# Expert activations of 48 tokens from gathered rows of u, those of 208 from dense products

## The chip, the cores and the metric

One core of one Trainium2 chip. The metric is the device time of one execution in microseconds (us), as a median of several runs. A profiled execution on the same core gives the trace.

## The reference

Two transformer blocks on 256 tokens of width 2048 (`D`), all in fp32. The change concerns the last part, the expert layer of the second block. For each token and each of 8 heads it picks 16 of 16384 experts (128 in all), and an expert is a row of `u_table` and a row of `v_table`, each of 2048 numbers:

```python
q = jnp.dot(h, w_pq)                      # per head two halves, scored against 128 keys each
v1, i1 = lax.top_k(s1, 16); v2, i2 = lax.top_k(s2, 16)
vals, ci = lax.top_k(v1 + v2 of all pairs, 16)
idx = i1[ci // 16] * 128 + i2[ci % 16]    # 128 experts of a token
g = jax.nn.softmax(vals, axis=-1)
a = jnp.einsum('td,tkd->tk', ht, u_table[idx])
w = jax.nn.gelu(a) * g
return jnp.einsum('tk,tkd->td', w, v_table[idx])
```

## The kernel before

Activations are kept transposed: features on partitions, the 256 tokens along the free dimension. A matrix is read in chunks of 512 KB by DMAs on SP's queue (`wload`, L335) into one of four raw buffers. ScalarE rounds a chunk to a high half (`wh`, L341), and VectorE forms the low half, the rest (`wl`, L342). The activations `xh` hold, for each group of 128 features, 256 columns of high halves and 256 of low halves. TensorE then forms, for each 128 x 128 piece of the matrix, a wide product of the high weights with all 512 columns (L367) and a narrow one of the low weights with the 256 high columns (L370), both added up in one bank of PSUM.

The expert layer (`peer`) doesn't look up rows. It computes the activation of every expert for every token: 128 blocks of u (`u_block`), each of 128 experts, of 16 pairs of a wide and a narrow product, out of two chunks. `addh` adds the two halves of the bank (ScalarE L425, VectorE L427), and ScalarE's gelu writes the block to the large tile A (blocks 0 to 63) or B (64 to 127), 128 partitions x 64 blocks x 256 tokens (L1416). Beside it VectorE finds the chosen experts (`select`: `top_keys`, `top_pairs`, `look`, `weights`), first for tokens 0 to 127, then for the others. `gates` turns the choice into a mask: for each token, two one-hot operands on VectorE (`oh` L1429, `og` L1431, the latter with the gate weight split into three bf16 pieces `gp`), three small products on TensorE (L1439), and for each group of 8 tokens a multiplication of the large tile by the result (L1442). Last, 256 chunks of v are multiplied with the masked tiles (L1489 to L1491).

Order: the program lists the instructions, with side work handed out in steps by `pump` (two steps a block of u): `select` beside blocks 0 to 63, `gates(A)` beside 64 to 127, `gates(B)` beside the product with v. A scheduler sets the order of each engine at compile time by priority and by when operands are expected. The conversions of weights (`wload`) have high priority. Each engine works through its queue in order. Pools hold a fixed number of buffers: three for high halves, two for low ones; tile B takes the place of what selection used.

An earlier stage (`ada`, L771) has the same multiply-and-sum instruction that the change uses, on rows of 1024.

## Time and profile before

| | |
|---|---|
| median of 3 runs | 3251.58 us (3250.17 to 3252.47) |
| profiled execution, its own time | 3250.42 us |
| its span in the trace | 3248.6 us |
| TensorE products busy | 98% |
| VectorE busy | 80% |
| ScalarE busy | 53% |
| GpSimd busy | 0% |
| mean rate of transfers | 210 GB/s |

Busy times are sums over the whole span; stages differ, so rows by stretch stand below. PE is TensorE's products, PEld its weight loads, DVE VectorE, ACT ScalarE, POOL GpSimd, SP the engine whose queue issues most DMAs. Products are pipelined and overlap: the time that one costs in a row of them is the distance between starts, not its length.

### The profile page before, as it was taken

To read this page: it belongs to the slowest core of one execution; us is meant where nothing else is said; L and a number is where in the kernel's file an instruction comes from. 1 tells how busy PE (TensorE), PEld (TensorE's weight loads), DVE (VectorE), ACT (ScalarE), POOL (GpSimd) and SP (SyncE) were. 2 spreads that over 40 slices of the span, in tenths; PEclk is the share of its full clock that TensorE was granted. 3 is DMA by queue.
4 is the path that set the end of the run, shared out by engine and by line. 5 is a ranking of instruction groups with operands and counts; after the bars stand their busy time and mean duration, and the time that the engine had idled before them with its cause. 6 is when DMAs were issued, how large, how long until landed. Compare 5 with 4: busy or idle time off the path is not lost.

```text
span 3248.6 us, 49371 instructions
## 1 busy us (share of the span) xinstructions
PE 3168.1 (98%) x18168; PEld 2710.0 (83%) x18168; DVE 2600.8 (80%) x4740; ACT 1712.2 (53%) x2599; POOL 11.1 (0%) x27
## 2 busy tenths in 40 slices
PE   8999899999999998999989999999999999999997
PEld 7888788888888887888878888888888888888886
DVE  6768888898999998668879965588888888875656
ACT  6676654444444666555655544444444444455553
POOL 0000000000000000000000000000000000000000
PEclk9999999999999998999989999999999999999999
DMA  6655589999999844554445555555555555565654
GB/s 236 204 175 188 171 286 332 326 330 331 326 331 327 290 150 139 175 176 156 143 151 171 183 188 186 187 176 176 176 176 169 181 176 181 178 219 194 194 194 149
DMA packets 187970, 682.05 MB, mean 210 GB/s; under 512 B 21344, under 2 KB 21728, under 8 KB 187088
## 3 DMA queue, kind: packets, MB, share of 16 engines
q1 hardware_dynamic: 185472, 671.97, 61.2%
q10 hardware_dynamic: 1440, 4.91, 0.4%
q8 instruction: 142, 2.33, 0.3%
q0 software_dynamic: 816, 2.03, 0.2%
q14 instruction: 100, 0.82, 0.1%
HBM read 673.44 MB, written 4.20 MB: 209 GB/s over the span
## 4 chain that ended last, share of the span: by engine, by line
PE 90%; DVE 8%; ACT 1%; issue 1%; DMA 1%; DVEq 0%; ACTq 0%; SPq 0%
PE bank L367 40%; PE bank L370 21%; PE bank L1489 7%; PE bank L1490 7%; PE bank L1491 7%; DVE wl L342 2%; PE bank L1439 1%; PE bank L412 1%; PE bank L413 1%; PE bank L414 1%; PE bank L658 0%; PE bank L629 0%; DVE t L1294 0%; ACT wh L341 0%; DMA raw<-w_ada 0%
## 5 line engine op out<-in xcount | busy, mean ns | idle before, releaser
L367 PE MATMUL bank<-xh,wh 128*128 128x512 f32 x5264 | 1741.7, 399 | 37.0 <-DVE xh L455 20.3
L342 DVE TENSOR_TENSOR wl<-raw,wh 128x1024 fp32r<-128x1024 f32 x1066 | 1302.6, 1223 | 561.5 <-issue 257.0
L341 ACT CAST wh<-raw 128x1024 fp32r<-128x1024 f32 x1067 | 1119.5, 1050 | 906.0 <-PE bank L367 762.9
L370 PE MATMUL bank<-xh,wl 128*128 128x256 f32 x5264 | 1295.5, 282 | 0.4 <-DVE wl L342 0.2
L367 PEld LDWEIGHTS bank<-xh,wh 128*128 128x128 f32 x5264 | 982.0, 189 | 251.6 <-issue 19.6
L370 PEld LDWEIGHTS bank<-xh,wl 128*128 128x128 f32 x5264 | 931.1, 190 | 19.8 <-DVE wl L342 3.8
L1489 PE MATMUL bank<-wh,xh 128*128 128x512 f32 x1020 | 404.4, 396 | 2.1 <-ACT xh L1482 2.0
L1491 PE MATMUL bank<-wh,xh 128*128 128x512 f32 x1020 | 398.1, 390 | 0.0
L1490 PE MATMUL bank<-wl,xh 128*128 128x512 f32 x1016 | 396.6, 390 | 0.0
L771 DVE CUSTOM_DVE_ANT_0 raw<-raw,crow 128x1024 f32<-128x1024 f32 x192 | 234.2, 1220 | 12.5 <-DMA raw<-w_ada 12.1
L1491 PEld LDWEIGHTS bank<-wh,xh 128*128 128x128 f32 x1020 | 191.8, 188 | 40.4 <-DVE xh L1483 0.2
L1489 PEld LDWEIGHTS bank<-wh,xh 128*128 128x128 f32 x1020 | 192.1, 188 | 39.9 <-ACT xh L1482 2.4
L1490 PEld LDWEIGHTS bank<-wl,xh 128*128 128x128 f32 x1016 | 191.5, 188 | 37.1
L1431 DVE SCALAR_TENSOR_TENSOR og<-iota,i1T,gp 128x192 bf16<-128x192 bf16 x512 | 211.2, 413 | 0.0
L367 PE MATMUL bank<-fx,wh 128*128 128x512 f32 x704 | 180.6, 393 | 0.0
L427 DVE TENSOR_TENSOR tmp<-bank,tmp 128x256 f32<-128x256 f32 x388 | 153.3, 420 | 11.0 <-ACT tmp L425 10.2
L1482 ACT CAST xh<-bigA 128x256 fp32r<-128x256 f32 x128 | 51.5, 406 | 189.7 <-PE bank L1490 189.0
L367 PEld LDWEIGHTS bank<-fx,wh 128*128 128x128 f32 x704 | 127.0, 189 | 23.3 <-DVE fx L903 0.2
L425 ACT COPY tmp<-bank 128x256 f32<-128x256 f32 x388 | 131.8, 372 | 22.6 <-PE bank L370 22.1
L1482 ACT CAST xh<-bigB 128x256 fp32r<-128x256 f32 x128 | 51.7, 409 | 162.9 <-PE bank L1490 162.9
L1429 DVE TENSOR_SCALAR oh<-iota,i2T 128x128 bf16<-128x128 bf16 x512 | 127.7, 249 | 0.0
L370 PE MATMUL bank<-fx,wl 128*128 128x256 f32 x704 | 103.9, 283 | 0.0
(414 smaller groups left out, 2296.2 us busy)
## 6 DMA issues: line engine op xcount, KB each, us to landing
raw<-u SPq DMA_DIRECT2D x256, 512.0 KB, 3.5
raw<-v SPq DMA_DIRECT2D x256, 512.0 KB, 3.5
raw<-w_ada SPq DMA_DIRECT2D x192, 512.0 KB, 5.2
raw<-w_gu SPq DMA_DIRECT2D x176, 512.0 KB, 5.2
raw<-w_in SPq DMA_DIRECT2D x144, 512.0 KB, 3.6
raw<-w_down SPq DMA_DIRECT2D x88, 512.0 KB, 5.3
raw<-w_out SPq DMA_DIRECT2D x32, 512.0 KB, 4.0
raw<-w_ple_gate SPq DMA_DIRECT2D x32, 512.0 KB, 3.5
```

Of the source, the lines that this page charges most:

```text
L341: nc.scalar.copy(H[:, :n], raw[:, :n])
L342: nc.vector.tensor_tensor(L[:, :n], raw[:, :n], H[:, :n].bitcast(F32), OP.subtract)
L367: self.nc.tensor.matmul(p, lhsT=H[:, kk, c], rhs=xh(k0 + kk), start=k0 + kk == 0, stop=False)
L370: self.nc.tensor.matmul(p[:, T:], lhsT=L[:, kk, c], rhs=xh(k0 + kk)[:, :T], start=False, stop=k0 + kk == nk - 1)
L425: self.nc.scalar.copy(out[:, j], p[:, T:])
L427: self.nc.vector.tensor_tensor(out[:, j], p[:, :T], out[:, j], OP.add)
L771: nc.vector.tensor_tensor_reduce(raw, raw, self.crow[:, h * 1024:h * 1024 + 1024], 1.0, 0.0, OP.mult, OP.add, s[:, h:h + 1])
L1429: nc.vector.tensor_scalar(oh, iota, i2T[:, t:t + 1], None, op0=OP.is_equal)
L1431: nc.vector.scalar_tensor_tensor(og, iota[:, hf * 64:hf * 64 + 64].unsqueeze(1).to_broadcast(shp), i1T[:, t:t + 1], gp[:, :, t:t + 1].to_b ...
L1489: nc.tensor.matmul(o, lhsT=wH, rhs=H[:, 0, c], start=first, stop=False)
L1490: nc.tensor.matmul(o, lhsT=wH, rhs=L[:, 0, c], start=False, stop=False)
L1491: return nc.tensor.matmul(o, lhsT=wL, rhs=H[:, 0, c], start=False, stop=last)
```

## The change

Tokens 0 to 47 leave the dense products of u. Both products of a pair then have 208 tokens: 416 columns wide and 208 narrow (`t0=NG`). The activations of the 48 tokens are computed for their 128 chosen experts alone. TensorE transposes the h of the first 128 tokens by 32 products with an identity, and it goes to DRAM (`hr`). When the first 128 tokens are selected, the expert numbers are laid out so that 128 partitions hold 32 tokens x 4 columns of choices, or 16 tokens x 8 (`GATHER`, `rows_of`, `by_part`). Each of 48 gathers on POOL's queue brings 128 rows of u (8 KB each, 1 MB), VectorE multiplies them with the rows of h of the same tokens and sums (`tensor_tensor_reduce`, 2048 columns), one gather at four of every seven blocks, from the end of the first selection. In the first half their buffers are tiles of their own, two for gathered rows; in the second they are parts of B that aren't yet written, two and later one. At the end (`gathered`) the sums go through gelu, are multiplied by the gate weights, go through DRAM into transposed form and are split into `gp`, in place of the bare gate weights, so that `gates` for these tokens (now taken last) copies instead of multiplying. `gp` becomes bf16.

```diff
+GATHER = ((0, 32), (32, 16))
+NG = 48
...
+    o["u_rows"] = u
...
-    def dense_t(self, chunks, xh, evac, nt=4, kc=KC, nw=512, hold=False):
+    def dense_t(self, chunks, xh, evac, nt=4, kc=KC, nw=512, hold=False, t0=0):
...
             if hold:
...
-            self.products(ps, self.wchunk(src, kc, nw), xh, c * kc, kc, nk)
+            self.products(ps, self.wchunk(src, kc, nw), xh, c * kc, kc, nk, t0)
             if c < len(chunks) - 1:
...
-    def products(self, ps, w, xh, k0, kc, nk):
+    def products(self, ps, w, xh, k0, kc, nk, t0=0):
...
+        n = T - t0
...
         def hi(j, p, kk, c):
-            self.nc.tensor.matmul(p, lhsT=H[:, kk, c], rhs=xh(k0 + kk), start=k0 + kk == 0, stop=False)
+            x = xh(k0 + kk)
+            if t0:
+                x, p = x.rearrange("p (s t) -> p s t", s=2)[:, :, t0:], p[:, :2 * n].rearrange("p (s t) -> p s t", s=2)
+            self.nc.tensor.matmul(p, lhsT=H[:, kk, c], rhs=x, start=k0 + kk == 0, stop=False)
         def lo(j, p, kk, c):
-            self.nc.tensor.matmul(p[:, T:], lhsT=L[:, kk, c], rhs=xh(k0 + kk)[:, :T], start=False, stop=k0 + kk == nk - 1)
+            self.nc.tensor.matmul(p[:, n:2 * n], lhsT=L[:, kk, c], rhs=xh(k0 + kk)[:, t0:T], start=False, stop=k0 + kk == nk - 1)
         for s in steps:
...
             if not self.grouped:
...
-    def addh(self, out, ps):
+    def addh(self, out, ps, n=T):
         for j, p in enumerate(ps):
-            self.nc.scalar.copy(out[:, j], p[:, T:])
+            self.nc.scalar.copy(out[:, j], p[:, n:2 * n])
         for j, p in enumerate(ps):
-            self.nc.vector.tensor_tensor(out[:, j], p[:, :T], out[:, j], OP.add)
+            self.added = self.nc.vector.tensor_tensor(out[:, j], p[:, :n], out[:, j], OP.add)
     def pair(self):
...
-            gp = sm.tile([128, 3, T], F32, name="gp", bufs=1)
+            gp = sm.tile([128, 3, T], BF, name="gp", bufs=1)
+            gi = [sm.tile([128, n], U32, name=f"gi{t}", bufs=1) for t, n in GATHER]
+            ga = [sm.tile([128, n], F32, name=f"ga{t}", bufs=1) for t, n in GATHER]
+            gg = [sm.tile([128, n], F32, name=f"gg{t}", bufs=1) for t, n in GATHER]
+            hr = self.dram.tile([128, D], F32, name="hr")
+            gw = self.dram.tile([NG, 128], F32, name="gw")
...
+            qc = ExitStack()
+            qp = qc.enter_context(tc.tile_pool(name="qp", bufs=2))
             for g in range(4):
-                q = tk.tile([128, 4, T], F32, name="q", bufs=2)
+                q = qp.tile([128, 4, T], F32, name="q")
                 if self.ps2:
...
+            idr = qp.tile([128, 128], F32R, name="idr", bufs=1)
+            nc.scalar.copy(idr, self.ident)
+            for q in range(4):
+                ps = self.bank()
+                for i in range(4):
+                    for s in range(2):
+                        nc.tensor.matmul(ps[:, i * 128:i * 128 + 128], lhsT=xh(4 * q + i)[:, s * T:s * T + 128],
+                                         rhs=idr, start=s == 0, stop=s == 1)
+                r = qp.tile([128, 512], F32, name="hq")
+                nc.scalar.copy(r, ps)
+                nc.gpsimd.dma_start(hr[:, q * 512:q * 512 + 512], r)
+            qc.close()
+            up = tkc.enter_context(tc.tile_pool(name="up", bufs=1))
             def top_keys(tt, h, half):
...
+            def by_part(g, src, dst):
+                t0, n = GATHER[g]
+                for c in range(128 // n):
+                    nc.gpsimd.dma_start(dst[c * n:c * n + n], src[t0:t0 + n, c * n:c * n + n])
+            def rows_of():
+                f = tk.tile([128, 128], F32, name="place")
+                nc.vector.scalar_tensor_tensor(f, sel[0], 128.0, sel[1], OP.mult, OP.add)
+                i = tk.tile([128, 128], U32, name="at")
+                nc.vector.tensor_copy(i, f)
+                for g in range(len(GATHER)):
+                    by_part(g, i, gi[g])
+            def pieces(src, c):
+                r = sm.tile([128, T], F32, name="tmp", bufs=2)[:, c]
+                nc.vector.tensor_copy(r, src)
+                for k in range(3):
+                    nc.vector.tensor_copy(gp[:, k, c], r)
+                    if k < 2:
+                        nc.vector.tensor_tensor(r, r, gp[:, k, c], OP.subtract)
             def weights(tt):
...
+                if tt == 0:
+                    for g in range(len(GATHER)):
+                        by_part(g, e.rearrange("p a b -> p (a b)"), gg[g])
...
-                r = tk.tile([128, 128], F32, name="gr")
-                b = tk.tile([128, 128], BF, name="gb")
-                nc.vector.tensor_copy(r, ps[:, 256:384])
-                for k in range(3):
-                    nc.vector.tensor_copy(b, r)
-                    nc.vector.tensor_copy(gp[:, k, c], b)
-                    if k < 2:
-                        nc.vector.tensor_tensor(r, r, gp[:, k, c], OP.subtract)
+                n = 0 if tt else NG
+                pieces(ps[:, 256 + n:384], slice(tt * 128 + n, tt * 128 + 128))
+            todo = [(g, s) for g, (t, n) in enumerate(GATHER) for s in range(n)]
+            def gather(n, home, held):
+                for g, s in todo[:n]:
+                    if g not in held:
+                        t0, m = GATHER[g]
+                        h = held[g] = home(f"hr{g}")
+                        for c in range(128 // m):
+                            nc.gpsimd.dma_start(h[c * m:c * m + m], hr[t0:t0 + m])
+                    r = home("ur")
+                    nc.gpsimd.indirect_dma_start(out=r, out_offset=None, in_=a["u_rows"],
+                                                 in_offset=bass.IndirectOffsetOnAxis(ap=gi[g][:, s:s + 1], axis=0))
+                    with tc.issue_after(self.added.ins):
+                        nc.vector.tensor_tensor_reduce(r, r, held[g], 1.0, 0.0, OP.mult, OP.add, ga[g][:, s:s + 1])
+                del todo[:n]
+            def gathered():
+                for g, (t0, n) in enumerate(GATHER):
+                    nc.scalar.activation(ga[g], ga[g], AF.Gelu)
+                    nc.vector.tensor_tensor(ga[g], ga[g], gg[g], OP.mult)
+                    for c in range(128 // n):
+                        nc.gpsimd.dma_start(gw[t0:t0 + n, c * n:c * n + n], ga[g][c * n:c * n + n])
+                yield
+                w = sm.tile([128, T], F32, name="tmp", bufs=2)[:NG, :128]
+                nc.gpsimd.dma_start(w, gw)
+                yield
+                ps = self.bank()
+                nc.tensor.transpose(ps[:, 0:NG], w, self.ident[:NG, :NG])
+                pieces(ps[:, 0:NG], slice(0, NG))
             def select():
                 for tt in range(2):
...
+                    if tt == 0:
+                        rows_of()
...
+                    ready.append(tt)
...
+            ready = []
             def u_block(b, dst):
                 def ev(ps):
-                    t = self.tmp()
-                    self.addh(t.unsqueeze(1), ps)
-                    nc.scalar.activation(dst, t, AF.Gelu)
-                self.dense_t([a["u"][b, c] for c in range(2)], xh, ev, nt=1, kc=8, nw=128)
+                    t = self.tmp()[:, NG:]
+                    self.addh(t.unsqueeze(1), ps, T - NG)
+                    nc.scalar.activation(dst[:, NG:], t, AF.Gelu)
+                self.dense_t([a["u"][b, c] for c in range(2)], xh, ev, nt=1, kc=8, nw=128, t0=NG)
             def gates(big, hf):
...
-                for tg in range(32):
+                for tg in [*range(NG // 8, 32), *range(NG // 8)]:
...
                     for k0 in (0, 4):
...
                         if k0:
...
-                            nc.vector.tensor_tensor(w, w, ps.rearrange("p t i -> p i t"), OP.mult)
+                            if tg * 8 < NG:
+                                nc.vector.tensor_copy(w, ps.rearrange("p t i -> p i t"))
+                            else:
+                                nc.vector.tensor_tensor(w, w, ps.rearrange("p t i -> p i t"), OP.mult)
...
+            held = {}
+            def home(name):
+                return up.tile([128, D], F32, name=name, bufs=2 if name == "ur" else 1)
             for b in range(64):
...
+                if ready and b * 4 % 7 < 4:
+                    gather(1, home, held)
...
+            held = {}
+            place = {"hr0": 32, "hr1": 56, "ur": 40}
+            def home(name):
+                k = place[name]
+                if name == "ur":
+                    place[name] = 48 if k == 40 or b > 34 else 40
+                return B[:, k:k + 8].rearrange("p a b -> p (a b)")
+            last = gathered()
             for b in range(64):
...
+                if b * 4 % 7 < 4:
+                    gather(1, home, held)
+                if b in (47, 48, 51):
+                    assert not todo
+                    next(last, None)
...
```

## Rows read from the trace of the kernel before

**Rows 1.** The page, part 1: busy time, share of the span, instructions of each engine.

```profile
PE 3168.1 (98%) x18168; PEld 2710.0 (83%) x18168; DVE 2600.8 (80%) x4740; ACT 1712.2 (53%) x2599; POOL 11.1 (0%) x27
```

**Rows 2.** Busy time by stretch, the columns as in its head line.

```profile
core 0: us, PE busy (x) PEld busy (x) DVE busy (x) ACT busy (x) POOL busy (x), PEclk, DMA share, GB/s
1754.00:2117.00 363.00, 362.83 (x2062) 314.20 (x2061) 255.21 (x530) 182.43 (x263) 0.00 (x0) 1.00 0.57 186
2117.00:2500.00 383.00, 380.96 (x2778) 329.17 (x2777) 316.03 (x737) 178.91 (x262) 0.00 (x0) 1.00 0.53 175
2500.00:3240.00 740.00, 731.69 (x3893) 598.09 (x3891) 559.17 (x1085) 352.34 (x520) 0.00 (x0) 1.00 0.56 185
...
1900.00:2117.00 217.00, 217.00 (x1241) 188.42 (x1240) 112.92 (x128) 107.37 (x154) 0.00 (x0) 1.00 0.58 187
```

**Rows 3.** The activations of the blocks of u (L1416): shortest, median, longest; first, last start.

```profile
L1416 ACT ACTIVATE bigA<-tmp x64: 417/418/422, 1754.6 to 2111.5; 128x256 f32<-128x256 f32 x64
L1416 ACT ACTIVATE bigB<-tmp x64: 414/418/418, 2117.3 to 2496.0; 128x256 f32<-128x256 f32 x64
```

**Rows 4.** Waits in the first half: total us, times, longest.

```profile
DVE wl L342 <- PE bank L370: 105.7, 77, 1.7
```

**Rows 5.** Timeline of TensorE within a block: start us, length us, engine, line.

```profile
2112.04 0.40 PE L367 MATMUL bank<-xh,wh 128*128 128x512 f32 x1
...
2112.28 0.28 PE L370 MATMUL bank<-xh,wl 128*128 128x256 f32 x1
2112.28 0.19 PEld L367 LDWEIGHTS bank<-xh,wh 128*128 128x128 f32 x1
2112.39 0.40 PE L367 MATMUL bank<-xh,wh 128*128 128x512 f32 x1
```

**Rows 6.** Timeline of TensorE and of its weight loads, products of 4 columns (L1220).

```profile
1606.57 0.95 PE L1220 MATMUL bank<-w,x 128*128 128x4 f32 x8
1607.38 0.48 PE L367 MATMUL bank<-xh,wh 128*128 128x512 f32 x1
...
1606.45 0.97 PEld L1220 LDWEIGHTS bank<-w,x 128*128 128x128 f32 x8
```

**Rows 7.** Busy time by two other stretches; columns as in rows 2.

```profile
500.00:900.00 400.00, 400.00 (x2295) 352.23 (x2295) 360.93 (x549) 185.27 (x244) 0.00 (x0) 1.00 0.91 329
...
1606.00:1608.00 2.00, 2.00 (x16) 1.86 (x15) 2.00 (x5) 1.05 (x1) 0.00 (x0) 1.00 0.77 205
```

**Rows 8.** The multiply-and-sum of an earlier stage (L771): shortest, median, longest ns.

```profile
L771 DVE CUSTOM_DVE_ANT_0 raw<-raw,crow x192: 1206/1220/1229, 59.3 to 1109.4; 128x1024 f32<-128x1024 f32 x192
L771 DVE DVE_READ_ACCUMULATOR2_ANT ada<- x192: 76/84/96, 60.5 to 1110.6; 128x1 f32 x192
```

**Rows 9.** VectorE's groups in the second half: busy us, mean ns of one.

```profile
L342 DVE TENSOR_TENSOR wl<-raw,wh 128x1024 fp32r<-128x1024 f32 x127 | 155.2, 1222 | 66.9 <-issue 65.7 <-PE bank L1490 1.1
L1431 DVE SCALAR_TENSOR_TENSOR og<-iota,i1T,gp 128x192 bf16<-128x192 bf16 x256 | 105.5, 412 | 0.0
L1429 DVE TENSOR_SCALAR oh<-iota,i2T 128x128 bf16<-128x128 bf16 x255 | 63.4, 249 | 0.0
L427 DVE TENSOR_TENSOR tmp<-bank,tmp 128x256 f32<-128x256 f32 x64 | 26.8, 418 | 0.1
L1442 DVE TENSOR_TENSOR bigA<-bigA,bank 128x512 f32<-128x512 f32 x32 | 21.8, 681 | 0.0
```

**Rows 10.** DMA issues: count, KB each, median us from issue to landing.

```profile
raw<-u SPq DMA_DIRECT2D x256, 512.0 KB, 3.5
...
bigA<-rows SPq DMA_DIRECT2D x2, 1024.0 KB, 6.7
...
swq<-qr POOLq DMA_DIRECT2D x4, 128.0 KB, 4.5
```

**Rows 11.** Timeline: eight records of plain fp32 products of 256 columns (L658).

```profile
108.69 1.97 PE L658 MATMUL bank<-xc,rgw 128*128 128x256 f32 x8
```

## What I predict, and why

> **What bounds the kernel now.** I read the page's engine totals first [rows 1]: TensorE is busy for 98% of the span, VectorE for 80%, and the reader should see that no other engine is near TensorE on average. The change acts only in the last of the three stages, so the second view is busy time by stretch [rows 2]. There are three stretches: the first 64 blocks of the expert table u (1754 to 2117 us, "first half"), the other 64 (2117 to 2500, "second half"), and the product with v (2500 to 3240). In all three TensorE has no gap worth naming and its granted clock is 1.00. VectorE has 255 us of work in the 363 us of the first half and 316 in the 383 of the second. The activations' own rows give the period of a block [rows 3]: (2111.5 - 1754.6)/63 = 5.67 us in the first half, (2496.0 - 2117.3)/63 = 6.01 in the second, where the gate products join in. The wait list of the first half says that VectorE's L342, the low halves of the weights, waits for TensorE and not the reverse [rows 4]. So a block costs what TensorE's own instructions take, until VectorE has more to do than TensorE.
>
> **Products.** A block is 16 pairs of one wide product (L367, 512 columns) and one narrow (L370, 256 columns). Starts in the timeline are 0.24 us apart after a wide one and 0.11 after a narrow one [rows 5]; 5.67/16 = 0.354 a pair, split two to one, is 0.236 and 0.118. The change makes them 416 and 208 columns. The wide one falls by 96/512 of 0.236, 0.044 us. The narrow one would fall by 0.022 if columns alone set it. It loads 128 weight columns for the next product all the same, and the trace shows what that costs in products of only 4 columns (L1220): eight weight loads occupy 0.97 us, so less the 0.19 of one they start 0.111 us apart; from the first of the products to the wide one behind the eighth it is 0.81, 0.101 each [rows 5, 6], at a granted clock of 1.00 [rows 7]. A product of hardly any columns thus costs 0.10 to 0.11, against 0.118 for 256. I take the narrow one at 0.118, unchanged, since the loads' spacing is so near it; the bounds are a gain of 0 and of 0.017 by these rows, and 0.022 by columns alone. A pair falls to 0.310, a block by 16 x 0.044 = 0.71 us, each half by 64 x 0.71 = 45 us. The Trainium skill, "TensorE: Matmul & The Clock Gate", section "Back-to-back issue gap", gives an isolated spacing of N/2.4 + 2.5 ns; by it the pair would fall by 60 ns, 123 us over 2048 pairs, an estimate from that page. The 4-column rows speak against using it here, and so does the same section, which says that it leaves out the weight load.
>
> **Rows of h.** Ahead of the first block there are 32 more products of 128 columns. At 0.10 to 0.118 each [rows 5, 6] they are 4 us on TensorE's path. Their four copies are on ScalarE, which is busy half of the first half [rows 2]: nothing.
>
> **VectorE.** Each of the 48 gathers adds a multiply-and-sum of 2048 columns. The same operation exists at L771: 1.22 us for 1024 columns, plus 0.08 to read the sum [rows 8]. The fixed part follows from L427 and L342, both tensor-tensor: (1222 - 418)/(1024 - 256) = 1.05 ns a column [rows 9], so 2048 columns take 1.22 + 1.07 + 0.08 = 2.37 us, of which some 0.08 overlaps the next: 2.29, or 110 us for all. Selection of the first 128 tokens ends in block 25 (two steps a block, 51 steps), and four blocks of seven then take one: blocks 25 to 63 hold 23, the second half's blocks 0 to 42 hold 25. First half: 255 + 23 x 2.29 - 3 (64 sums 48 columns shorter) = 305 us, in 363 - 45 + 4 = 322. In its later part, where there is room before, 113 us of 217 [rows 2] become 166 of some 190. It fits. Second half: 316 + 25 x 2.29 - 3 + 3 (splitting and scaling the gathered sums) = 373 us, where TensorE would need 383 - 45 = 338. It doesn't fit: VectorE becomes the bound of the second half, and 373 is the least it can take. The gates' operands (L1431, L1429) are also VectorE's, and the product with v needs every gate, so nothing of it can be put off beyond the half. I take 375, a gain of 8 instead of 45. Bf16 gate weights might make L1431 shorter; 0 to 0.16 us each (down to the 0.25 of L1429), up to 256 x 0.16 = 41 us. I take 0: its own row is the nearest, and one value is still spread over 64 columns. The 12 multiplications replaced by copies read the same PSUM: nothing either way.
>
> **Transfers.** Block pace and gathers together ask, in blocks 25 to 63, for 39 x 1.05 MB + 23 x 1.05 + 1.05 for the rows of h = 66 MB in 39 x 4.96 = 193 us, 342 GB/s. The trace sustains 329 at a DMA share of 0.91 with TensorE at 100% [rows 7]. 66 MB at 329 take 201 us: 0 to 8 us more, I take 5. In the second half the pace is lower and there is room. The DMAs are on POOL's queue, which had nothing to do (11 us busy in all [rows 1]); nothing of SP's is moved.
>
> **Waits.** The multiply-and-sum stands on VectorE's in-order queue and waits for its gather. Behind it stand the next block's low halves (L342), and TensorE waits for those, with two buffers of cover, about 2 us. Two gather buffers give a gather 2 x 7/4 blocks, 17 us. Landing times are 3.5 us for a 512 KB load of u and 6.7 for 1 MB on SP's queue, and 4.5 for a small load on POOL's [rows 10]; sharing the engines, I estimate about 10 us. So it is hidden in the steady state. The start of each half (the rows of h are loaded again) and the end, where one buffer remains, may show some us: 0 to 10, I take 3. New small transfers at the end (the gathered sums by way of DRAM) have three blocks, 15 us, of cover.
>
> **Sum.** First half -45 + 4 + 5 = -36; second half -8; starts +3; product with v 0. That is -41 against the profiled execution of 3250.4 us: 3209. The profile lies 1.2 us under the median, so 3210.
>
> **Rivals.** *Columns decide, and VectorE keeps up* (bf16 gate weights do shorten L1431): both halves fall by 45, 3250 - 90 + 4 = 3164; with the narrow product falling too, 3251 - 135 + 4 = 3120. For it: VectorE lacks only 35 us. Against: the 4-column rows. Chance 0.12.
> *Gathers land late*: slower. Each gather asks POOL for 128 addresses, and its data shares engines near their limit. If it takes longer than the 17 us between two uses of a buffer, VectorE stands in front of L342 and TensorE behind it. It outweighs the gain from 41/48 = 0.9 us a gather; at 2.5 us beyond cover it costs 120 and gives 3330, at 1.5 us 3282. Against: the 10 us above. The Trainium skill, "SBUF — State Buffer", section "SBUF: two separate sides", has a rule that would bring it about: while VectorE runs a two-port operation, GpSimd can't write its descriptors. No row here shows a gather, and VectorE is to be nearly always busy. Chance 0.17.
> *Transfers limit more*: at 300 GB/s in the first half 220 instead of 201 us, 3210 + 22 = 3232. Chance 0.13.
> *It does not gain what it takes*: each block of the second half waits for its own gates, so that the 43 gather blocks run at 316/64 + 25 x 2.29/43 = 6.3 us of VectorE instead of 6.01 (+12) and starts show 10 to 20 us: about 3245 to 3250. Chance 0.07.
> *Narrow products run slowly.* No row has a rounded-fp32 product of under 256 columns other than these slots. Plain fp32 ones of 256 columns take two records of about 0.23 [rows 11], four times the narrow slot's rate a column; at that rate 208 columns cost 0.38, +0.26 x 2048 = 530 us, 3780. Chance 0.03.
>
> **Chances and range.** Forecast 0.48 (3195 to 3225 by its bounds), rivals as given. What this kernel's measurement can tell from no change is 0.2%, 6.5 us: faster means under 3245. Faster 0.48 + 0.12 + 0.13, less some late gathers among them: 0.71. Same 0.08. Slower 0.21. The range takes in the first rival and the slow transfers and stops short of late gathers at 1.5 us each: 3160 to 3265.
>
> **What would show it.** Block periods of about 4.96 us in the first half and 5.8 on average in the second; 4-column spacing in narrow products (0.11 to 0.12); VectorE at 99% of the second half; L342 waiting no more for TensorE there. It is wrong if VectorE shows waits for a gather, if the narrow slot is 0.096 us, as columns alone would have it, or over 0.2, or if TensorE stays at 99% in the second half.

## The result, and the profile after

The changed kernel takes 3279.63 us (median of 4 runs, 3272.45 to 3284.80) against 3251.74 for the kernel before beside it: a ratio of 1.0085, with a 95% interval of 1.0065 to 1.0104. It is 28 us slower, where 41 us less was forecast. The profiled execution took 3284.8 us (span 3283.0), 34.4 us more than that of before, so the sums below go by 34 us. Beside [rows 1] the page shows TensorE at 95% instead of 98%; 2600.8 us of VectorE have become 2699.8, near the 48 sums' 113.

```profile
PE 3119.2 (95%) x18201; PEld 2728.7 (83%) x18201; DVE 2699.8 (82%) x4840; ACT 1702.2 (52%) x2605; POOL 104.6 (3%) x132
```

The activations of the blocks of u, now L1506, answer [rows 3]: duration ns (shortest/median/longest), first and last start.

```profile
L1506 ACT ACTIVATE bigA<-tmp x64: 376/378/379, 1764.5 to 2129.6; 128x208 f32<-128x208 f32 x64
L1506 ACT ACTIVATE bigB<-tmp x64: 376/378/382, 2134.5 to 2529.2; 128x208 f32<-128x208 f32 x64
```

The first start is 9.9 us later than before. The first half takes 365.1 instead of 356.9, the second 394.7 instead of 378.8, and what follows 755.6 instead of 754.4. With 0.9 less between the halves that is 34 us. Both halves lose, and in different ways. Busy time by stretch, columns as in [rows 2]: the first ten blocks, the rest of the first half, the start of the second, its blocks with gathers, its end.

```profile
core 0: us, PE busy (x) PEld busy (x) DVE busy (x) ACT busy (x) POOL busy (x), PEclk, DMA share, GB/s
1765.00:1847.00 82.00, 58.05 (x289) 51.86 (x288) 81.79 (x278) 25.81 (x39) 13.59 (x26) 0.85 0.44 142
1847.00:2129.00 282.00, 271.18 (x1726) 262.94 (x1724) 201.74 (x234) 145.37 (x216) 35.16 (x21) 0.98 0.76 278
2135.00:2171.00 36.00, 26.23 (x200) 25.09 (x198) 23.86 (x49) 10.77 (x16) 9.42 (x11) 0.91 0.98 286
2171.00:2421.00 250.00, 218.15 (x1690) 205.69 (x1691) 239.74 (x495) 105.08 (x158) 24.94 (x27) 0.97 0.73 253
2421.00:2500.00 79.00, 78.89 (x638) 76.30 (x638) 73.91 (x179) 39.32 (x58) 4.06 (x9) 0.98 0.63 200
```

In the first 82 us TensorE works 58 while VectorE has no gap: the place that was to be the easiest is the worst, and no gathered row has been summed yet (the first sum starts at 1926). After it TensorE is busy for 96%, and until the gathers begin a block takes 4.83 us (4.96 forecast). From 2171 to 2421 VectorE is busy for 96% and TensorE for 87%: there VectorE is the bound, as forecast, though not at the forecast price.

**The first ten blocks.** TensorE's timeline within the first block (start us, length us, engine, line; in brackets the idle time before and its releaser):

```profile
1753.43 0.37 PE L375 MATMUL bank<-xh,wh 128*128 128x416 f32 x1
1753.63 0.25 PE L378 MATMUL bank<-xh,wl 128*128 128x208 f32 x1
1753.73 0.37 PE L375 MATMUL bank<-xh,wh 128*128 128x416 f32 x1
1759.81 0.54 PE L378 MATMUL bank<-xh,wl 128*128 128x208 f32 x1 [5.71 <-DVE wl L345]
1760.15 0.59 PE L375 MATMUL bank<-xh,wh 128*128 128x416 f32 x1
1760.53 0.38 PE L378 MATMUL bank<-xh,wl 128*128 128x208 f32 x1
1760.71 0.59 PE L375 MATMUL bank<-xh,wh 128*128 128x416 f32 x1
```

A pair takes 0.30 us. Then TensorE stands 5.71 us for VectorE's low halves (L345). After the gap pairs take 0.56 us until 1765. VectorE's own timeline tells what it did instead:

```profile
1758.52 1.23 DVE L345 TENSOR_TENSOR wl<-raw,wh 128x1024 fp32r<-128x1024 f32 x1
1759.65 0.77 DVE L1400 TENSOR_TENSOR eq<-eq,xf 128x256 f32<-128x256 f32 x2
1760.32 0.75 DVE L1401 TENSOR_REDUCE sel<-eq 128x16 f32<-128x256 f32 x2
1760.98 0.76 DVE L1398 TENSOR_TENSOR eq<-wf,io 128x256 f32<-128x256 f32 x2
1761.65 0.77 DVE L1400 TENSOR_TENSOR eq<-eq,xf 128x256 f32<-128x256 f32 x2
1762.32 0.75 DVE L1401 TENSOR_REDUCE sel<-eq 128x16 f32<-128x256 f32 x2
1762.97 1.23 DVE L345 TENSOR_TENSOR wl<-raw,wh 128x1024 fp32r<-128x1024 f32 x1
```

Between two conversions stand ten selection instructions (x2 is two of them), so a chunk takes 4.45 us and a block nearly 9. The periods in the timeline of L1506 are 8.94, 8.53, 9.63, 9.36, 9.75, 9.67, 9.04, 8.62, 8.86, then 5.19, 5.13 and 4.83. The wait list of 1754 to 1900 (total us, times, longest) is that of [rows 4] turned round: there VectorE's low halves waited for TensorE.

```profile
PEld bank L378 <- DVE wl L345: 35.1, 18, 6.0
PE bank L378 <- DVE wl L345: 29.7, 18, 5.7
```

That order was fixed at compile time. Instructions on VectorE's queue between two conversions, from the first chunk of u on, counted in the compiled programs (the last three kernels are experiments below):

```
before                           10   6   6   8   6   6   6   5   5   5   5
changed (narrow 208)             46  10  10  12   9  10  14  13  12  12  12
48 tokens, narrow 256            39   5   5   3   5   4   4   4   6   4   4
16 tokens, narrow 256            39   7   4   5   4   5   5   6   5   5   4
16 tokens, narrow 240            48  12  14  12  11  18  13  16  13  16  14
```

The narrow product doesn't account for all of it. The first number, the instructions ahead of the first conversion of u, is 39 with narrow products of 256 columns too. In the kernel whose products stay as before (gathers alone, below) the trace, counted in the same way, has 40 there and then 5 or 6. TensorE waits in the first block of these two kernels as well (256 columns with 48 tokens, then gathers alone):

```profile
1761.11 0.38 PE L378 MATMUL bank<-xh,wl 128*128 128x256 f32 x1 [3.75 <-DVE wl L345]
1758.63 0.39 PE L378 MATMUL bank<-xh,wl 128*128 128x256 f32 x1 [3.25 <-DVE wl L345]
```

So some 2 of the 5.71 us belong to the shorter product, and the rest to another part of the change. That part isn't the gathers or the sums: with 256 columns and neither of them, the wait is 3.76 us. Which part it is was not tried.

**The second half.** VectorE's groups from 2171 to 2421 (busy us, mean ns of one, idle time before them), beside [rows 9]:

```profile
L345 DVE TENSOR_TENSOR wl<-raw,wh 128x1024 fp32r<-128x1024 f32 x78 | 95.0, 1225 | 6.4 <-PE bank L378 4.0 <-issue 2.3
L1521 DVE SCALAR_TENSOR_TENSOR og<-iota,i1T,gp 128x192 bf16<-128x192 bf16 x156 | 65.3, 419 | 0.0
L1466 DVE CUSTOM_DVE_ANT_0 bigB<-bigB 128x2048 f32<-128x2048 f32 x23 | 52.6, 2286 | 1.9 <-DMA bigB<-u_rows,gi 1.9
...
L1466 DVE DVE_READ_ACCUMULATOR2_ANT ga<- 128x1 f32 x23 | 2.0, 85 | 0.0
```

The sum costs 2.29 + 0.08 us, as worked out, it hardly waits for its gather (1.9 us), and bf16 gate weights don't shorten L1521. Gathers land in time; from the DMA issues (count, median us from issue to landing, of the five and six gathers whose landing the trace has):

```profile
bigB<-u_rows,gi POOLq DMA_INDIRECT x25, 5.6
ur<-u_rows,gi POOLq DMA_INDIRECT x23, 8.6
```

The start of the half is the exception. In the timeline of all engines, rows of h (L1461) are loaded again around the first two gathers (L1463). The first, issued at 2134.87, is ready at 2147.33, 12.5 us later; VectorE stands for it, and TensorE behind VectorE:

```profile
2134.87 1.00 POOL L1463 DMA_INDIRECT bigB<-u_rows,gi  x1 [0.30 <-issue]
...
2136.17 2.23 POOL L1463 DMA_INDIRECT bigB<-u_rows,gi  x1 [0.30 <-issue]
...
2138.39 0.55 POOL L1461 DMA_DIRECT2D bigB<-hr  x1
...
2147.33 2.29 DVE L1466 CUSTOM_DVE_ANT_0 bigB<-bigB 128x2048 f32<-128x2048 f32 x1 [5.36 <-DMA bigB<-u_rows,gi]
...
2150.83 0.54 PE L378 MATMUL bank<-xh,wl 128*128 128x208 f32 x1 [6.86 <-DVE wl L345]
```

The late gather alone doesn't make this loss. ScalarE also waits there for a chunk of u, 5.25 us until 2145.39. In the kernel that keeps the sums and the loads of rows of h but has no gathers (below), it waits 7.08 and 5.85 us for chunks, and the first four periods take 35.5 us; here they take 36.1.

### The profile page after: what moved, and what is told of

It reads as the page before. It is cut to its first block, busy times and chain, and to the rows that moved or that the text cites. A ratio compares the mean times of both kernels' runs of the same rounds, so it can differ in the third digit from the quotient of the medians.

```text
span 3283.0 us, 49729 instructions
## 1 busy us (share of the span) xinstructions
PE 3119.2 (95%) x18201; PEld 2728.7 (83%) x18201; DVE 2699.8 (82%) x4840; ACT 1702.2 (52%) x2605; POOL 104.6 (3%) x132
## 3 DMA queue, kind: packets, MB, share of 16 engines
HBM read 726.94 MB, written 5.28 MB: 223 GB/s over the span
## 4 chain that ended last, share of the span: by engine, by line
PE 85%; DVE 10%; DMA 3%; ACT 1%; issue 1%; DVEq 0%; POOL 0%; SPq 0%; ACTq 0%; POOLq 0%
PE bank L375 38%; PE bank L378 19%; PE bank L1603 7%; PE bank L1604 7%; PE bank L1605 7%; DVE wl L345 3%; PE bank L1529 1%; DMA raw<-u 1%; PE bank L420 1%; PE bank L421 1%; PE bank L422 1%; DVE og L1521 1%; DMA bigB<-u_rows,gi 1%; ACT wh L344 1%; DVE oh L1519 0%
## 5 line engine op out<-in xcount | busy, mean ns | idle before, releaser
L375 PE MATMUL bank<-xh,wh 128*128 128x512 f32 (+1 forms) x5264 | 1672.9, 392 | 36.9 <-DVE xh L463 19.8
L345 DVE TENSOR_TENSOR wl<-raw,wh 128x1024 fp32r<-128x1024 f32 x1066 | 1302.5, 1224 | 474.0 <-issue 206.6
L378 PE MATMUL bank<-xh,wl 128*128 128x256 f32 (+1 forms) x5264 | 1266.2, 276 | 55.1 <-DVE wl L345 54.3
L375 PEld LDWEIGHTS bank<-xh,wh 128*128 128x128 f32 x5264 | 995.2, 191 | 172.1 <-issue 19.5
L378 PEld LDWEIGHTS bank<-xh,wl 128*128 128x128 f32 x5264 | 948.4, 193 | 88.2 <-DVE wl L345 72.5
L1521 DVE SCALAR_TENSOR_TENSOR og<-iota,i1T,gp 128x192 bf16<-128x192 bf16 x512 | 212.7, 416 | 0.1
L435 DVE TENSOR_TENSOR tmp<-bank,tmp 128x256 f32<-128x256 f32 (+1 forms) x388 | 147.5, 404 | 29.1 <-ACT tmp L433 28.1
L433 ACT COPY tmp<-bank 128x256 f32<-128x256 f32 (+1 forms) x388 | 126.6, 359 | 22.4 <-PE bank L378 21.9
```

Of the source, the lines that this page charges most:

```text
L345: nc.vector.tensor_tensor(L[:, :n], raw[:, :n], H[:, :n].bitcast(F32), OP.subtract)
L375: self.nc.tensor.matmul(p, lhsT=H[:, kk, c], rhs=x, start=k0 + kk == 0, stop=False)
L378: self.nc.tensor.matmul(p[:, n:2 * n], lhsT=L[:, kk, c], rhs=xh(k0 + kk)[:, t0:T], start=False, stop=k0 + kk == nk - 1)
L433: self.nc.scalar.copy(out[:, j], p[:, n:2 * n])
L435: self.added = self.nc.vector.tensor_tensor(out[:, j], p[:, :n], out[:, j], OP.add)
L1521: nc.vector.scalar_tensor_tensor(og, iota[:, hf * 64:hf * 64 + 64].unsqueeze(1).to_broadcast(shp), i1T[:, t:t + 1], gp[:, :, t:t + 1].to_b ...
```

## Experiments

All kernels in one table, in us. Stretches are differences of starts of the blocks' activations, in each kernel's profiled execution: the first 9 periods, the 54 that follow, the second half (63), and its first 43, in which the 48-token kernels gather. "16 first" gathers in the first half, "16 second" in the second; "24 first" is the kernel with 24 tokens.

```
                        median  ratio    start   9    54    second  its 43
before                  3251.7   -      1754.6  50.4 306.5  378.8   258.5
changed                 3279.6  1.0085  1764.5  82.4 282.7  394.7   287.2
e2 products, 208        3206.3  0.9862  1768.7  82.6 262.6  332.8   226.7
e3 products, 256        3179.8  0.9780  1767.9  42.9 269.6  341.5   232.6
e1 narrow 256           3254.3  1.0013  1767.0  42.4 277.7  409.1   296.8
e4 gathers only         3289.5  1.0118  1761.7  52.1 305.5  409.2   287.8
e6 e1, one column       3199.5  0.9839  1765.5  42.8 273.2  357.2   248.9
e8 e1, sums only        3248.6  0.9991  1767.0  42.2 272.6  407.2   297.8
e5 32 tokens            3225.8  0.9920  1765.1  44.4 284.4  373.8   261.3
e12 32, faster rate     3229.8  0.9941  1766.4  44.3 291.9  361.5   249.0
e9 16 first             3227.3  0.9931  1764.0  48.7 290.8  365.9   249.5
e10 16 second           3248.9  0.9997  1761.7  48.6 293.3  384.7   268.3
e11 16 first, 240       3256.3  1.0016  1767.5  85.2 284.7  357.5   243.8
e7 24 first             3250.2  0.9998  1769.0  46.3 314.6  364.5   248.3
```

**Products alone, narrow at 208 and at 256 columns.** The first takes gathers and sums out of the changed kernel; the second also gives the narrow products all 256 columns (in a bank laid out for 512) and the first wide product of a block 512.

```diff
-                    r = home("ur")
-                    nc.gpsimd.indirect_dma_start(out=r, ...)
-                    nc.vector.tensor_tensor_reduce(r, r, held[g], ..., ga[g][:, s:s + 1])
+            for t in ga:
+                nc.vector.memset(t, 0.0)
```
```diff
-            self.nc.tensor.matmul(p[:, n:2 * n], lhsT=L[:, kk, c], rhs=xh(k0 + kk)[:, t0:T], ...)
+            self.nc.tensor.matmul(p[:, T:], lhsT=L[:, kk, c], rhs=xh(k0 + kk)[:, :T], ...)
```

> The changed kernel without the 48 gathers and their sums (zeros stand for the sums, so that the 48 tokens get no expert output); products of 416 and 208 columns. Theory (order): the slow first ten blocks stay (+41 us against 4.83 a block), as they need no gather; the remaining first half at 4.83, the second half bound by TensorE at about 5.2 a block: 3195 to 3210 us. Rival (gathers and their transfers slow the first half): the first half runs at 4.83 from the start, 3155 to 3170.

> As the run without gathers, but with the narrow product at 256 columns (again without expert output for 48 tokens). Theory (order): some 30 us faster than with 208 columns although each narrow product is longer, since the first ten blocks run at pace: 3160 to 3180 us, blocks of about 4.96 in the first half. Rival (order plays no part): about 16 us slower than with 208 columns, 2048 pairs by up to 0.01 us.

The second saves 71 us: 44 in the first half (312.5 for 356.9), 37 in the second, less 13 for its late start. Without gathers the first nine periods with 208 columns stay at 82.6, against 42.9 with 256: the loss there belongs to the products and not to the gathers. Between the two kernels the narrow product's columns, the place of the results in the bank and the first wide product of a block change together, and they were not tried apart. Past the first blocks the shorter narrow product is the faster one, 262.6 against 269.6 for 54 periods: 0.13 us a block. Of it 0.04 is the first wide product, which has 96 columns more in the second kernel, so 0.005 a narrow product is left. The second half adds 8.7 us to its favour, and it still ends 26.5 us behind. The same stretch of the kernel with 256 columns, as in the first row of the busy times above:

```profile
1765.00:1847.00 82.00, 81.97 (x516) 79.46 (x515) 81.34 (x230) 43.88 (x65) 11.62 (x24) 0.98 0.66 207
```

TensorE is full with VectorE as busy as there. VectorE's work is the same; only its order differs.

**The changed kernel with narrow products at 256.** Only the second of the two diffs.

> The change, with the narrow product left at all 256 columns (the wide one stays at 416, the first of a block at 512). In the changed kernel the selection on VectorE stands 9 to 13 instructions thick between two weight conversions where it was 4 to 6, and the first ten blocks take about 9 us instead of 4.83. Theory (order): the scheduler counted a block with a narrow product of 208 columns as about twice as long as it is and filled the gap; at 256 columns the order is that of before again, the first ten blocks take about 5 us, the first half ends some 35 to 40 us earlier, the whole takes 3225 to 3245 us. Rival (VectorE simply has too much to do once TensorE is faster): the first ten blocks stay near 9 us, and since a narrow product of 256 columns is a little longer the whole takes 3280 to 3296. In the second half both expect about 6.1 us a block while gathers run.

3254.3, 25 us less than the changed kernel and level with the one before, but not the 3225 to 3245 that I expected. The first nine periods are 42.4. The second half is worse than in the changed kernel, 409.1 for 394.7; why was not tried. Against the same products without gathers (341.5), 25 gathers cost 67.6 us there, 2.7 each, and the 23 of the first half 7.6, 0.3 each (320.1 for 312.5).

**Gathers alone.** All 256 tokens stay in the products, and the 48 tokens' activations come from the gathers as before.

```diff
-                self.dense_t([a["u"][b, c] for c in range(2)], xh, ev, nt=1, kc=8, nw=128, t0=NG)
+                self.dense_t([a["u"][b, c] for c in range(2)], xh, ev, nt=1, kc=8, nw=128)
```

> The changed kernel with dense products for all 256 tokens (512 and 256 columns as before), the gathers and their use as in the change: what the added work costs by itself. Theory: TensorE stays the bound of the first half, which costs only the 4 us of the 32 extra products; the second half shows the start of its gathers, about 12 us, and VectorE at 373 us of work just under TensorE's 383: 3262 to 3280 us. Rival (gathers are hidden behind a full set of products): 3252 to 3258. Rival (each gather holds VectorE up): over 3300.

It takes 3289.5, more than the 3262 to 3280 expected. With TensorE at its old pace the 23 gathers of the first half cost 0.7 us together (357.6 for 356.9), those of the second 30.4, 1.2 each. TensorE's slower blocks of 6.01 hide more of VectorE's extra work there; its first four periods already take 3 us more.

**The sum or the transfer.** Two kernels from the one with 256 columns: in one the sum becomes a copy of one column, with the gathers kept; in the other the gathers are left out and the sums kept, on the rows of h that are loaded.

```diff
-                        nc.vector.tensor_tensor_reduce(r, r, held[g], 1.0, 0.0, OP.mult, OP.add, ga[g][:, s:s + 1])
+                        nc.vector.tensor_copy(ga[g][:, s:s + 1], r[:, 0:1])
```
```diff
-                    nc.gpsimd.indirect_dma_start(out=r, ..., in_=a["u_rows"], ...)
-                        nc.vector.tensor_tensor_reduce(r, r, held[g], ...)
+                        nc.vector.tensor_tensor_reduce(r, held[g], held[g], ...)
```

> As the run of the whole change with the narrow product at 256 columns (3254 us), with all gathers, but in place of each multiply-and-sum of 2048 columns VectorE only copies one gathered column (the 48 tokens' expert weights are then meaningless). Theory (the second half pays for VectorE's 2.3 us a gather, behind which the gates' operands and the weight conversions stand while TensorE's queue waits in order): most of the 68 us by which the second half exceeds the one without gathers goes, 3190 to 3215 us, and the start of the second half stays slow by some 10 to 15. Rival (the transfers of 25 MB beside those of u): 3240 to 3255.

> As the run of the whole change with the narrow product at 256 columns (3254 us), with the 48 multiply-and-sums but without the 48 gathers (each sum takes the rows of h twice, so that the 48 tokens' expert weights are meaningless); the rows of h are still loaded. Theory (VectorE): the second half stays near 6.5 us a block on average, 3230 to 3254 us. Rival (transfers): 3180 to 3205.

Without the gathers the second half stays at 407.2 (409.1 with them); without the sums it falls to 357.2, and without either it was 341.5. So most of the price in the second half is VectorE's 2.3 us and not the 26 MB. Of the 16 us that the gathers cost with one column, 10 fall in the first six periods (42.3 against 32.4). The stretch 2171 to 2421 of the kernel with 256 columns, whole, and then with one column for the sum:

```profile
2171.00:2421.00 250.00, 222.70 (x1637) 203.35 (x1636) 226.78 (x476) 101.20 (x151) 33.68 (x30) 0.94 0.65 229
```
```profile
2171.00:2421.00 250.00, 248.99 (x2018) 238.98 (x2017) 226.24 (x551) 122.72 (x185) 22.07 (x29) 1.00 0.77 261
```

With the sums, VectorE is busy for 91% and TensorE for 89%: neither is full, they wait for each other in turn. Without them TensorE is full while more is transferred. Between 2117 and 2421 the wait list of the whole kernel has TensorE stand 30 us for the gates' operand:

```profile
PE bank L1529 <- DVE og L1521: 30.1, 18, 3.4
```

**16 tokens, gathers in one half or the other.** Narrow products at 256; the 16 gathers all fall in the first half, or by leaving out the first half's call all in the second.

```diff
-GATHER = ((0, 32), (32, 16))
-NG = 48
+GATHER = ((0, 16),)
+NG = 16
```
```diff
-                if ready and b * 4 % 7 < 4:
-                    gather(1, home, held)
```

> 16 tokens instead of 48, narrow products at 256 columns, all 16 gathers in the first half behind the first selection, one set of rows of h. Wide products 480 columns: 32/512 of 0.236 us on 2048 pairs, 30 us less; rows of h 4 us more. My theory (a gather is nearly free in the first half, where VectorE has room): 0 to 5 us for the gathers, so 3224 to 3231, and blocks of about 5.45 us in both halves' steady parts. Rival (a gather costs 2.3 us or more wherever it stands, as the sum does on VectorE): 16 x 2.3 = 37 us more, 3261. Rival (the beginnings cost most: place, loads of rows of h): the second half clean, but 10 to 20 us lost at the first gather, 3240.

> The same 16 tokens with the same 16 gathers, all in blocks 0 to 27 of the second half. My theory (what a gather costs is decided by the half: VectorE's queue there also holds the gates' operands that TensorE waits for): 2.7 us for each by the 48-token kernels (68 us for 25), 43 us, and the second half's first blocks at 7 to 9 us: 3262 to 3272. Rival (a gather's price doesn't depend on the half): the time of the kernel with all gathers in the first half, within 5 us.

The same work, 3227.3 and 3248.9: the place alone makes 22 us. In the first half the gathers cost nothing that shows, and the kernel beats the changed one and the one before (0.9931, 0.9914 to 0.9947). In the second I expected 2.7 us each and measured 18.8 / 16 = 1.2. So a gather has no fixed price. The least that the gathers can cost is what VectorE's block exceeds TensorE's by. With 16 tokens TensorE's block is 5.81 there, and the gathers' 28 blocks take 6.45; VectorE's share, 316/64 [rows 2] + 16 x 2.37/28 = 6.29, bounds them: 28 x 0.48 = 13 of the 19 us. The same sum over 43 blocks gives 45 of 62 us in the changed kernel (394.7 against 332.8 without gathers), 39 of 68 with 256 columns and 13 of 30 for the gathers alone. The rest is lost at the start and in waits of the engines for each other, and was not separated further. Busy times from 2110 to 2290, gathers in the first half and then in the second:

```profile
2110.00:2290.00 180.00, 180.00 (x1368) 162.50 (x1367) 153.38 (x357) 85.96 (x125) 0.00 (x0) 1.00 0.57 182
```
```profile
2110.00:2290.00 180.00, 173.16 (x1225) 148.01 (x1224) 172.66 (x349) 77.58 (x113) 23.50 (x14) 0.98 0.68 245
```

**The same 16 tokens, narrow products at 240 columns.**

```diff
-            self.nc.tensor.matmul(p[:, T:], lhsT=L[:, kk, c], rhs=xh(k0 + kk)[:, :T], ...)
+            self.nc.tensor.matmul(p[:, n:2 * n], lhsT=L[:, kk, c], rhs=xh(k0 + kk)[:, t0:T], ...)
```

> The kernel with 16 tokens and all gathers in the first half, the narrow products at 240 columns instead of 256, nothing else. By the compile-time order VectorE's queue now has 48 instructions ahead of the first low halves and then 11 to 18 between two conversions, where the kernel with 256 columns has 39 and then 4 to 7. My theory (the order of VectorE's queue turns at once when the narrow product has fewer than 256 columns, however few are taken): the first eight to nine blocks of u at 9 to 11 us instead of 5.4, 30 to 45 us more there, less some 2 us for the shorter products: 3250 to 3270. Rival (what slows the first ten blocks of the changed kernel comes with its 48 tokens or its gathers, or the number of columns acts gradually): within 5 us of 3227.

29 us slower than with 256 columns. The first nine periods take 85.2 instead of 48.7 (10.15, 10.64, 11.02, ...), though the shorter products save 6 us in the 54 that follow and 8 in the second half. It is not a matter of degree: 16 columns fewer, with the results' place in the bank that goes with them, turn the order as much as 48 (the table of counts above).

```profile
1765.00:1847.00 82.00, 58.05 (x256) 48.16 (x256) 81.71 (x280) 23.97 (x36) 9.65 (x18) 0.82 0.39 130
```

**Other numbers of tokens.** 32 tokens with 23 gathers in the first half; 32 with five gathers in seven blocks instead of four; and 24 tokens at five in seven, all in the first half, where two sets of rows of h share one buffer. All with narrow products at 256.

```diff
-GATHER = ((0, 32), (32, 16))
-NG = 48
+GATHER = ((0, 32),)
+NG = 32
```
```diff
-                if ready and b * 4 % 7 < 4:
+                if ready and b * 5 % 7 < 5:
```
```diff
-GATHER = ((0, 32), (32, 16))
-NG = 48
+GATHER = ((0, 16), (16, 8))
+NG = 24
...
-                return up.tile([128, D], F32, name=name, bufs=2 if name == "ur" else 1)
+                return up.tile([128, D], F32, name=name[:2], bufs=2 if name == "ur" else 1)
...
-                if ready and b * 4 % 7 < 4:
+                if ready and b * 5 % 7 < 5:
```

> The change with 32 tokens in place of 48 and the narrow product at 256 columns: 32 gathers, 23 in the first half and 9 in the second. Wide products of 448 columns: by 0.236 x 64/512 x 1024 = 30 us less in each half. Theory (a gather costs 0.3 us in the first half, 68/25 = 2.7 in the second): 3251 - 60 + 4 + 7 + 25 to 35 = 3227 to 3240 us, below before. Rival (what a gather costs is the same in both halves, about 1.5): 3251 - 60 + 4 + 48 = 3243 or more.

> The 32-token kernel (256-column narrow products, one set of rows of h) with five gathers in seven blocks of the first half instead of four: 28 of the 32 there, four left for the second half instead of nine. My theory (a gather costs 2 to 3 us in the second half and little in the first): first half up to 4 us more, since 1.80 MB a block at the 343 GB/s of the kernel with this rate take 5.25 us against 5.15; second half 8 to 12 us less: 3217 to 3223. Rival (the second half's loss is the restart, the reload of the rows of h and the first two gathers, not the gathers' number): within 4 us of the 3226 of the four-in-seven kernel. Rival (transfers at this rate come late, as in the kernel with 24 tokens and 5.35 us a block): 39 x 0.2 = 8 us more in the first half, about 3226 as well, but with blocks of 5.35.

> The change with 24 tokens, the narrow product at 256 columns and all 24 gathers in the first half (five of seven blocks take one, none is left for the second half). Wide products of 464 columns: 0.236 x 48/512 x 1024 = 23 us less in each half. Theory (gathers are nearly free where VectorE has room, and the second half's price is that of gathers beside gates): 3251 - 45 + 4 + 6 to 12 = 3214 to 3224 us, the fastest of the runs that compute all tokens. Rival (gathers cost about 1.5 us anywhere): 3251 - 45 + 4 + 36 = 3246.

32 tokens give 3225.8 (0.990 to 0.994), faster than the changed kernel and the one before. The faster rate moves five gathers into the first half: the second half is 12.3 us shorter, 2.5 each, and the first 7.4 longer, twice what I allowed. Its median, 3229.8 (3224.0 to 3236.3), is not better. The 24-token kernel was a miss: 3250.2 (0.9989 to 1.0008), with 3214 to 3224 expected. Its second half is clean (364.5 us), but the first takes 361. Blocks 49 to 51 (7.08, 10.87, 7.59) stand beside the exchange of the rows of h, whose 16 small loads go out one by one between 2022 and 2036; near the end three take 10.62, 17.17 and 15.83, with six of the last gathers one after another, each waited for by its sum. This timeline of POOL shows the end of the exchange (L1461):

```profile
2034.25 0.52 POOL L1461 DMA_DIRECT2D hr<-hr  x1 [0.82 <-DMA hr<-hr]
2035.24 0.52 POOL L1461 DMA_DIRECT2D hr<-hr  x1 [0.48 <-DMA hr<-hr]
2036.29 0.99 POOL L1463 DMA_INDIRECT ur<-u_rows,gi  x1 [0.53 <-DMA hr<-hr]
```

## Why the prediction was wrong

*Products: right in the sum, not in its split.* Before the gathers a block takes 4.83 us (4.96 forecast), so a pair falls by 0.052 us, from 0.354 to 0.302, where I took 0.044. But I had named a narrow slot of 0.096 us as a sign of being wrong. By the starts between 1855 and 1915 it is 0.095, and the wide product's slot is 0.207 instead of the 0.192 of its columns (0.10 and 0.20 in the timeline of the first block above). With a narrow product of 256 columns, the slots are 0.117 and 0.191, a pair of 0.307. So the 48 columns gain 0.005 us, inside my bounds of 0 and 0.017, and what a slot shows is not what a product adds to the pair. The estimate of 60 ns from the isolated spacing in the Trainium skill ("TensorE: Matmul & The Clock Gate", section "Back-to-back issue gap") is 8 more than the trace's 52, as far off as my 44.

*Rows of h: right.* The first wide product of u starts at 1748.85 instead of 1745.63.

*VectorE's first half, "it fits": the step that failed.* The sum over the half fits. But I took the order of VectorE's queue as given, and the change turned it: 46 and then 9 to 14 instructions ahead of a conversion instead of 10 and then 5 to 8. With narrow products of 256 columns it is 39 and then 3 to 7. All selection of the first ten blocks moves forward, TensorE waits for low halves, and later blocks have less to do. Nine periods take 82.4 where 9 x 4.96 = 44.6 was forecast, 38 us; with the 5.7 us in the first block that is 44 of the 75 us between the forecast -41 and the measured +34. Some 3.8 of the 5.7 come with 256 columns as well, so the products' part is 40. No rival named it. That the shorter narrow product, with its place in the bank, turns the order is shown (208 and 240 against 256, with gathers and without). How the scheduler comes to it was not tested; its operands' expected times are a likely cause and no more.

*Transfers: mis-sized.* I allowed 5 us. Gathers cost 282.7 - 262.6 = 20 us in the changed kernel's later first half, near the rival "transfers limit more" (22), but only 8 with 256 columns (277.7 - 269.6), with the same bytes. ScalarE's wait for chunks of u from 1847 to 2129 is the row that points to transfers. It is as long with 256 columns (29.8). What differs is that TensorE then stands for low halves, 12.2 us against 1.9:

```profile
ACT wh L344 <- DMA raw<-u: 27.1, 22, 4.4
...
PE bank L378 <- DVE wl L345: 12.2, 6, 3.4
```

At the longest of these stands ScalarE first waits 4.4 us for a chunk; then a sum of 2.28 us, at 2025.73, is on VectorE's queue ahead of the two conversions, and TensorE starts again at 2029.22. Why such waits of ScalarE don't reach TensorE with 256 columns is open.

*VectorE's second half: the bound was right, its size wrong.* I spread 373 us of VectorE over all 64 blocks, 5.83 each. The sums lie in 43 of them, and a block's own conversions and gate operands can't be put off to the last 21. VectorE asks 316/64 + 25 x 2.37/43 = 6.32 us in a gather block; from the fifth on they took (287.2 - 36.1)/39 = 6.44, and the last 20 periods 5.37 at TensorE's pace. That adds 8 us to the forecast's 369 for 63 periods, 6.44 for 6.32 another 5, the last 20 at 5.37 for 5.28 two more. The remaining 11 is the start: four periods of 5.23, 12.78, 6.74 and 11.39 for 25 us of work. My rival "it does not gain what it takes" is this mechanism, with 6.3 us a block and 10 to 20 for the starts. I gave it 0.07, because I let a sum over the half decide where the block does.

*Gathers land late: rightly refused in the steady state.* 8.6 and 5.6 us stand against 17 of cover, and leaving the gathers out gives back 2 us of the second half (narrow products at 256). Once, at the start of the half, one came late (12.5 us). That the measured 3280 lies beside this rival's 3282 is chance. The Trainium skill's rule ("SBUF — State Buffer", section "SBUF: two separate sides"), that VectorE's two-port operations keep GpSimd from writing descriptors, doesn't show as a delay here: gathers land in 5.6 us with VectorE busy for 96% of that stretch. Whether any of VectorE's instructions there is such an operation, no run shows.

*Starts, +3:* 11 us in the second half alone. *Product with v, 0:* 1.2 us.

*Sum.* Forecast -41, measured +34: the order of the queue 44 (40 of it from the products), transfers and other stalls in the later first half 10, the block-wise bound of the second half 13 and its end 2, the start of the second half 11, less 3 allowed, and small terms.

## What to carry to other kernels

Where a scheduler orders in-order queues at compile time, a new shape on one engine can reorder another engine: compare the compiled order of every queue before pricing the edit, and try the edit with the old shape (here a narrow product of 256 columns, 25 us). Bound a stage by its blocks, not by its sum, when work can't be put off across them; the bound is a least value, and the runs here lie 6 to 29 us above it. Put added work in the stretch where its engine has room: 16 gathers cost nothing to speak of in the first half and 19 us in the second, and with them there 16 tokens give 0.993 where 48 gave 1.0085.

## What the runs showed of the hardware

After TensorE had stood 5.7 us, its granted clock was 0.50 from 1760 to 1765 (1.2 instead of 2.4 GHz) and pairs took 0.56 us; after the next three waits, of 1.2 to 1.8 us, they took 0.30. At the lower level nine pairs took 0.26 us more each, 2.3 us. VectorE had no gap meanwhile, so it is not shown that the kernel lost them. From 1782.5 on the clock falls again, to 0.54 between 1795 and 1800, without another wait as long as the first (1.8 us before 1781.73, 2.25 before 1791.36); over the 82 us of the first stretch it is 0.85.

```profile
1760.00:1765.00 5.00, 5.00 (x18) 4.85 (x19) 5.00 (x14) 1.24 (x3) 0.00 (x0) 0.50 0.49 134
1795.00:1800.00 5.00, 3.82 (x15) 3.73 (x16) 5.00 (x21) 0.78 (x2) 1.77 (x2) 0.54 0.69 231
```

Transfers are not limited to the 329 GB/s that I took as a ceiling [rows 7]: gathers and chunks of u together reach 414 in a stretch of 5 us.

```profile
2020.00:2025.00 5.00, 5.00 (x35) 4.93 (x34) 1.23 (x1) 0.87 (x1) 0.00 (x0) 1.00 1.01 414
2025.00:2030.00 5.00, 1.56 (x8) 1.27 (x8) 4.56 (x5) 2.90 (x6) 1.67 (x1) 0.83 0.11 44
```

The burst is followed by 5 us with 44 GB/s while TensorE stands. In that time the next gather waits for the sum of 2025.73 (it is issued at 2028.30). Which of them brings about the other was not tried.
